# Two output projections done as one product of 2x2 blocks by seven multiplications

## The chip, the cores and the metric

The kernel runs on one core of one Trainium2 chip. The metric is the device time of one execution in microseconds (us), as the median of several runs. The profile shows the engines of the core: TensorE (PE for its matmuls, PEld for its weight loads), VectorE (DVE), ScalarE (ACT), GpSimd (POOL) and SyncE (SP, whose queue issues DMAs). SBUF is the working memory with 128 partitions, and PSUM is the memory of eight banks into which TensorE writes.

## The reference

One layer of a decoder trunk over 2048 positions of 1024 features, all in float32:

```python
h = rms_norm(x, norm1_g)
proj = einsum('bsd,dc->bsc', h, w_in)              # 2048 columns
a_out = spatial_gating(u_a, v_a, ...)              # 512 features
b_out = conformer_conv(val_b, gate_b, ...)         # 512 features
mix = concatenate([a_out, b_out], axis=-1)
x = x + einsum('bsc,cd->bsd', mix, w_out)          # the output projection
h = rms_norm(x, norm2_g)
f = square(relu(einsum('bsd,df->bsf', h, w_ff1)))  # 4096 features
x = x + einsum('bsf,fd->bsd', f, w_ff2)
return rms_norm(x, final_g)
```

The change is about the line of the output projection: a product of `mix` (2048 positions by 1024 features) with `w_out` (1024 by 1024), to which the residual `x` is added.

## The kernel before

**Tiles.** Activations lie transposed, with features on the partitions and positions along the free dimension. The positions are cut into four blocks of 512, numbered 0 to 3. Features and weight columns are cut into tiles of 128, so a block has 8 feature tiles (`KD`).

**Precision.** Every float32 operand is split into a high part, cast by ScalarE to a reduced form (fp32r), and a low part, which is the operand less its high part. A product of two split operands is three matmuls (`mm3`, line 179): high by high, high by low, low by high. The low part is computed by `rest` (line 163). It goes to GpSimd or to VectorE, whichever the kernel's own planner picks. The planner is a set of clocks, one for each engine, that advance by an assumed cost per instruction. `rest` takes GpSimd as long as its clock is less than `GPS_LEAD[0]` ahead of TensorE's clock, or more than 2 behind VectorE's. `GPS_LEAD` is 5.0 at first and 1.5 from line 1045.

**Memory.** Nearly all operands live in one pool of 41 slots of 128 x 1024 float32 (`slot`, `slot2`); smaller temporaries live in a pool of ten (`tmp`). An instruction that writes a new tile waits until a slot is free. DMAs are issued mostly by the queue of SyncE, in order.

**Order.** The changed stages stand under `manual_schedule`, so each engine gets its instructions in the order in which the program text makes them. Work that is to come some steps later is put into a list by `later(n, f)` and made by `beat()`, which is called once a step. `beside()` and `tick()` put bits of other work (such as the preparation of the down projection's weights, W2) beside a step: `pace["w2"]` says how many W2 items are begun for each call. An item is one prepared weight operand: a sum on VectorE (for four kinds in seven), a cast on ScalarE, a low part, and a DMA to DRAM.

**Stages.** The input projections and mixers of the four blocks come first, with the output projections of blocks 0 and 1 between them (`stage_o(0)`, `stage_o(1)`). The mixer's results of blocks 2 and 3 are stored in DRAM (`p_d`). Then come:

- u0, the first matrix of the MLP for blocks 0 and 1 together (`multiply("u0", ...)`, 112 steps);
- `stage_o(2)` and `stage_o(3)`, the output projections of blocks 2 and 3;
- u1, the same as u0 for blocks 2 and 3;
- the second matrix of the MLP, in 16 chunks (`down_chunk`).

u0, u1 and the down chunks already multiply by seven products. Two blocks of positions and two halves of the contracted and of the output features make a 2x2 by 2x2 block product. Seven products of sums of blocks give it, in place of eight. `BANK` (line 775) says in which bank a product is accumulated, and `INTO` (line 778) to which output block the bank's content is added when the product is done. The operands of u0 and u1 that come from the residual stream are called hops (`hop`, line 922): 28 slots for each pair of blocks, each made from `xr`, the residual after the output projection, by a scaling or a sum, a cast and a low part.

**The output projection of one block** (`stage_o`, line 645) runs over 8 output tiles `d`. Each takes one PSUM bank and contracts 8 feature tiles, 3 matmuls each: 192 matmuls of 128x128 weights by 512 positions. Weight tiles of 1024 columns come from `w_o` through `load_w`, `w_hi` and `w_lo`, two output tiles ahead. Both blocks load and split all of them. The mixer's results are brought back by `reload` (line 1007) and split into `mix[b]`. The result is added to the residual by VectorE (`evict`), stored as `x1_d`, and squared by ScalarE, and the squares are summed by GpSimd (`square_add`) for the second norm (`row_scale`). Beside `stage_o(2)`, 16 calls of `beside` with a pace of 0.2 make W2 items; beside `stage_o(3)` the hops of products 1, 2, 5 and 6 of u1 are made (`first_at`).

## Time and profile before

| What | Value |
|---|---|
| Median of 3 runs | 1831.97 us (1828.97 to 1837.33) |
| Profiled execution, its own time | 1831.89 us |
| Its span, first to last instruction | 1830.2 us |
| Granted TensorE clock, mean | 0.997 of full speed |
| DMA traffic | 424.74 MB, 232 GB/s over the span |

Lines of a group view read: line of the program, engine, operation, tile written <- tiles read, shapes, count | busy us, mean ns of one | idle time of the engine just before, and what ended it. Line 78 is the helper through which the planner's engines issue, so groups are told apart by their tiles: `po` is the bank of the output projection, `py`, `pz`, `px` are those of the seven-product stages, `w_hi`, `w_lo`, `m_hi`, `m_lo` the split operands. In the view of waits, a line gives who waited, for whom, us in total, times, and the longest. Matmuls are pipelined, so their durations overlap.

### The profile page before, as it was taken

To read this page: it belongs to the slowest core of one execution; us is meant where nothing else is said; L and a number is where in the kernel's file an instruction comes from. 1 tells how busy PE (TensorE), PEld (TensorE's weight loads), DVE (VectorE), ACT (ScalarE), POOL (GpSimd) and SP (SyncE) were. 2 spreads that over 40 slices of the span, in tenths; PEclk is the share of its full clock that TensorE was granted. 3 is DMA by queue.
4 is the path that set the end of the run, shared out by engine and by line. 5 is a ranking of instruction groups with operands and counts; after the bars stand their busy time and mean duration, and the time that the engine had idled before them with its cause. 6 is when DMAs were issued, how large, how long until landed. Compare 5 with 4: busy or idle time off the path is not lost. (4 is left out here: it accounts for less than half of the span.)

```text
span 1830.2 us, 23249 instructions
## 1 busy us (share of the span) xinstructions
PE 1809.3 (99%) x8080; PEld 1488.5 (81%) x8080; DVE 1330.8 (73%) x1825; ACT 758.6 (41%) x1172; POOL 1233.3 (67%) x775
## 2 busy tenths in 40 slices
PE   9999999999999999999999999999999999999998
PEld 6888878888888888888888888888788888888886
DVE  5699997997998985632567787676866568665655
ACT  6345565454445445455354545432322231212112
POOL 4575975883766666699878989776945465444434
PEclk9999999999999999999999999999999999999999
DMA  8342655432645456685557778998987679767652
GB/s 327 112 164 91 229 178 213 184 125 83 220 150 189 161 195 202 215 293 204 208 184 266 270 258 298 355 408 335 412 326 248 252 272 327 299 238 256 254 191 93
DMA packets 131686, 424.74 MB, mean 232 GB/s; under 512 B 14576, under 2 KB 15216, under 8 KB 131568
## 3 DMA queue, kind: packets, MB, share of 16 engines
q1 hardware_dynamic: 96000, 329.12, 50.5%
q10 hardware_dynamic: 35568, 94.13, 13.2%
q8 instruction: 64, 1.05, 0.2%
q14 instruction: 54, 0.44, 0.1%
HBM read 302.60 MB, written 120.59 MB: 231 GB/s over the span
## 5 line engine op out<-in xcount | busy, mean ns | idle before, releaser
L78 PE MATMUL py<-fo_hi,w2o 128*128 128x512 f32 x1792 | 555.9, 391 | 0.8 <-DVE x L78 0.8
L78 POOL TENSOR_TENSOR fo_lo<-fraw,fo_hi 128x1024 fp32r<-128x1024 f32 x111 | 274.4, 2481 | 252.9 <-ACT fo_hi L160 210.7
L78 DVE TENSOR_TENSOR x<-py,x 128x512 f32<-128x512 f32 x448 | 300.9, 687 | 185.8 <-PE py L78 185.4
L78 PEld LDWEIGHTS py<-fo_hi,w2o 128*128 128x128 f32 x1792 | 337.1, 188 | 72.0 <-DVE x L78 1.2
L78 PE MATMUL py<-hop,w1o 128*128 128x512 f32 x1536 | 363.8, 390 | 0.5 <-ACT c L982 0.4
L78 PE MATMUL py<-fo_lo,w2o 128*128 128x512 f32 x896 | 349.7, 390 | 0.9 <-POOL fo_lo L78 0.8
L78 PEld LDWEIGHTS py<-hop,w1o 128*128 128x128 f32 x1536 | 287.6, 188 | 62.4 <-issue 1.4
L78 DVE SCALAR_TENSOR_TENSOR acc<-g,vec,acc 128x512 f32<-128x512 f32 x464 | 322.9, 746 | 1.2
L160 ACT CAST fo_hi<-fraw 128x1024 fp32r<-128x1024 f32 x112 | 117.0, 1052 | 413.7 <-PE py L78 218.0
L78 POOL TENSOR_TENSOR w_lo<-raw,w_hi 128x1024 fp32r<-128x1024 f32 (+1 forms) x94 | 224.1, 2392 | 53.9 <-ACT w_hi L160 39.6
L78 POOL TENSOR_TENSOR w1o<-wraw,w1o 128x512 fp32r<-128x512 f32 x120 | 172.0, 1438 | 55.6 <-ACT w1o L810 43.4
L78 PEld LDWEIGHTS py<-fo_lo,w2o 128*128 128x128 f32 x896 | 168.6, 188 | 37.9 <-POOL fo_lo L78 2.6
L78 PE MATMUL pz<-hop,w1o 128*128 128x512 f32 x768 | 183.8, 390 | 0.0
L78 POOL TENSOR_TENSOR w1o<-ws,w1o 128x512 fp32r<-128x512 f32 x90 | 128.7, 1433 | 66.4 <-ACT w1o L810 62.6
L78 PEld LDWEIGHTS pz<-hop,w1o 128*128 128x128 f32 x768 | 143.8, 188 | 29.8
L78 DVE TENSOR_TENSOR fraw<-fraw 128x1024 f32<-128x1024 f32 x64 | 93.1, 1455 | 13.3 <-POOL fo_lo L78 13.2
L993 ACT ACTIVATE c<-c 128x512 f32<-128x512 f32 x128 | 80.8, 631 | 52.5 <-DVE c L78 52.0
L78 PE MATMUL po<-m_hi,w_hi 128*128 128x512 f32 x256 | 101.1, 395 | 0.0
L78 PE MATMUL po<-m_hi,w_lo 128*128 128x512 f32 x256 | 99.8, 390 | 0.6 <-POOL w_lo L78 0.6
L78 PE MATMUL po<-m_lo,w_hi 128*128 128x512 f32 x256 | 99.7, 389 | 0.0
L78 DVE TENSOR_TENSOR px<-px,c 128x512 f32<-128x512 f32 x32 | 22.3, 698 | 100.9 <-PE px L78 67.8
L78 POOL TENSOR_TENSOR w2p<-wraw,w2p 128x512 fp32r<-128x512 f32 x64 | 93.5, 1463 | 2.6 <-ACT w2p L810 2.6
(155 smaller groups left out, 2947.9 us busy)
## 6 DMA issues: line engine op xcount, KB each, us to landing
w2o<-w_d SPq DMA_DIRECT2D x224, 512.0 KB, 6.0
w_d<-w2p ACTq DMA_DIRECT2D x112, 512.0 KB, 5.4
wraw<-in_w SPq DMA_DIRECT2D x92, 512.0 KB, 4.7
f_d<-c ACTq DMA_DIRECT2D x128, 256.0 KB, 4.1
fraw<-f_d SPq DMA_DIRECT2D x64, 512.0 KB, 6.8
raw<-in_w_ct SPq DMA_DIRECT2D x48, 512.0 KB, 5.0
raw<-in_w_o SPq DMA_DIRECT2D x32, 512.0 KB, 5.4
w1o<-w_d SPq DMA_DIRECT2D x28, 512.0 KB, 5.5
```

What stands on the lines that cost most here:

```text
L78: return op(out, *args, **kwargs)
L160: nc.scalar.copy(hi, src)
L993: later(1, lambda: nc.scalar.activation(c, c, AF.Square))
```

## The change

`stage_o(2)`, `stage_o(3)`, `reload` and what belongs to them are taken out. In their place stands one loop, `stage_o_pair`, which computes both blocks as a product of 2x2 blocks by seven products. It takes its weights from a second arrangement of the same matrix, `w_o2`. The rows of the 2x2 are the parities of the feature tiles, the columns the two blocks (`t` = 0 is block 3, `t` = 1 is block 2). The contraction over four pairs of feature tiles, `q`, is the inner loop: step `n` is product `i` and depth tile `q`, 28 steps, in each of which all four output tiles `j` of the product get 12 matmuls. PSUM is reopened with all eight banks before the loop, and again as six and two after it.

```diff
-    def reload(b):
...
+    ORDER_O = (1, 5, 6, 3, 7, 2, 4)
+    OP = [(i, q) for i in ORDER_O for q in range(4)]
+    DONE = {3: (0, 1), 7: (1, 1), 2: (0, 0), 4: (1, 0)}
...
+    def op_hi(n):
+        if not 0 <= n < len(OP):
+            return
+        i, q = OP[n]
+        while ("m", q, 0 if i == 1 else 1) not in op:
+            op_load()
+        r11, r12 = [op["w", q, 0][:, a * 512:a * 512 + 512] for a in range(2)]
+        if i != 1:
+            r21, r22 = [op["w", q, 1][:, a * 512:a * 512 + 512] for a in range(2)]
+            if i == 5 and q % 2 == 0:
+                op["s", q // 2] = slot("osum")
+            s = op["s", q // 2][:, q % 2 * 512:q % 2 * 512 + 512]
+            if i == 5:
+                dsb.tensor_tensor(s, r21, r22, op=ALU.add)
+            elif i == 6:
+                dsb.tensor_tensor(s, s, r11, op=ALU.subtract)
+            elif i == 3:
+                dsb.tensor_tensor(s, r12, s, op=ALU.subtract)
+            elif i == 7:
+                dsb.tensor_tensor(r21, r11, r21, op=ALU.subtract)
+        lsrc = r11 if i == 1 else {2: r12, 4: r22, 5: s, 6: s, 3: s, 7: r21}[i]
+        bt = [op["m", q, t] for t in range(2 if i != 1 else 1)]
+        if i == 1:
+            rsrc = bt[0][:, :512]
+        else:
+            rsrc = right([[t[:, a * 512:a * 512 + 512] for t in bt] for a in range(2)], i, 0)
+        for side, src in (("l", lsrc), ("r", rsrc)):
+            o = slot2("of")
+            nc.scalar.copy(o[:, 0, :], src)
+            op[side, n] = (src, o)
+
+    def op_lo(n):
+        if 0 <= n < len(OP):
+            for side in "lr":
+                src, o = op[side, n]
+                rest(src, o[:, 0, :], o[:, 1, :])
+
+    def op_out(i, j, ps):
+        a, t = INTO[i]
+        b, d = 3 - t, 2 * j + a
+        x_ = xr[b][d]
+        dve.tensor_tensor(x_, ps, x_, op=ALU.add)
+        if DONE.get(i) == (a, t):
+            nc.sync.dma_start(
+                x1_d[b, j][:, a * 512:a * 512 + 512], xt1[b][j][:, a * 512:a * 512 + 512])
...
+    def stage_o_pair(at):
+        bks = {}
+        for n, (i, q) in enumerate(OP):
+            kind, first = BANK[i]
+            op_lo(n + 3)
+            op_hi(n + 4)
+            op_load()
+            ol, orr = op["l", n][1], op["r", n][1]
+            for j in range(4):
+                if first and q == 0:
+                    bks[kind, j] = mm_tile("po")
+                ps = bks[kind, j]
+                mm3(ps, [ol[:, k, j * P:(j + 1) * P] for k in range(2)],
+                    [orr[:, k, :] for k in range(2)], first and q == 0, q == 3)
+                if q == 3 and n == 27:
+                    op_out(i, j, ps)
+                elif q == 3:
+                    later(1, lambda j=j, ps=ps, i=i: op_out(i, j, ps), True)
+            beat()
+            at(n)
+
+    def at_o(n):
+        if 20 <= n < 24:
+            hop(1, 1, n - 20)
+        if 22 <= n < 26:
+            hop(1, 2, n - 22)
+        if n >= 26:
+            hop(1, 5, 2 * n - 52)
+            hop(1, 5, 2 * n - 51)
+        if n == O_LEAD[0]:
+            GPS_LEAD[0] = O_LEAD[1]
+        if n == 27:
+            GPS_LEAD[0] = 1.5
...
-    mid = reopen_banks(early, "m", mm=6, tp=2)
+    mid = reopen_banks(early, "o", mm=8)
...
-        stage_o(2, at_o2)
...
-        stage_o(3, first_at(1))
+        stage_o_pair(at_o)
+    mid = reopen_banks(mid, "m", mm=6, tp=2)
```

The function `right`, which was there for the down projection, makes the sum on the right side (one subtraction for products 5, 6, 7 and 4, in place). `op_load` issues the 24 loads of 512 KB (8 of weights, 8 of mixer results, 8 of the residual) on the queue of SyncE. It is called twice a step from step 102 of u0 on, and once a step in the loop. In the last four steps of u0 the operands of steps 0 to 3 are made.

`O_LEAD` is (14, -6.0): from step 14 to step 27 the planner's lead for GpSimd is -6.0, so that `rest` goes to VectorE unless GpSimd's clock is well behind. The hops of product 6 move from `stage_o(3)` into the first steps of u1 (`REST`, now one list for each pair of blocks). W2 items that were begun are finished in the first steps of the loop, and none is begun in it. `row_scale` gets two arguments for its delays.

More of the change, by code (lines that the diff above doesn't have):

```diff
@@ L149, in tp_tile @@
     def tp_tile(name):
-        return bank("tp", name)
+        return bank("tp" if "tp" in banks else "mm", name)
     def tiny(name, n=4):
@@ L1005, in reopen_banks @@
         return st
-    def reload(b):
-        p = parts[b]
-        g = p.reload()
-        def load(n):
-            while p.pairs[n] is None:
-                next(g)
-                if p.pairs[n] is None:
-                    yield
-        yield from load(0)
-        yield
-        yield from load(1)
-        yield
-        for k in range(KD):
-            if k % 2 == 0:
-                pair = halves(act_pair("m"))
-                yield from load(min(k // 2 + 2, 3))
-            nc.scalar.copy(pair[k % 2][0], p.at[k])
-            later(1, lambda k=k, hl=pair[k % 2]: rest(p.at[k], *hl))
-            mix[b].append(pair[k % 2])
-            yield
     def at_up0(n):
@@ L1102, in right, with op_loads, w, m @@
         return {1: b11, 2: b21, 5: b11, 6: b11, 7: b12, 3: b22, 4: b11}[i]
+    ORDER_O = (1, 5, 6, 3, 7, 2, 4)
+    OP = [(i, q) for i in ORDER_O for q in range(4)]
+    op = {}
+    DONE = {3: (0, 1), 7: (1, 1), 2: (0, 0), 4: (1, 0)}
+    def op_loads():
+        def w(q, a):
+            op["w", q, a] = slot("oraw")
+            nc.sync.dma_start(op["w", q, a], w_o2[q, a])
+        def m(q, t):
+            op["m", q, t] = slot("mraw")
+            nc.sync.dma_start(
+                op["m", q, t].rearrange("p (a t) -> p a t", a=2), p_d[1 - t, q])
+        for t in range(2):
+            for q in range(4):
+                w(q, t)
+                yield
+                m(q, t)
+                yield
+            for q in range(4):
+                load_resid(3 - t, q)
+                yield
@@ new lines, in hybrid_block_kernel, with op_load @@
+    op_gen = op_loads()
+    def op_load(n=1):
+        for _ in range(n):
+            next(op_gen, None)
+    def op_hi(n):
[28 more added lines that the diff above has]
+            op[side, n] = (src, o)
@@ new lines, in hybrid_block_kernel @@
+    count = [0, 0]
+    def stage_o_pair(at):
[18 more added lines that the diff above has]
+            at(n)
@@ new lines, in hybrid_block_kernel, with load_x1 @@
+    GPS_LEAD[0] = 1.5
+    dve.time += BEHIND
+    with tc.manual_schedule():
+        stage_o(1, first_at(0))
+        multiply("u0", UNITS, 0, up_out(0), at_up0)
+    mid = reopen_banks(early, "o", mm=8)
+    del banks["tp"]
+    gst.close()
+    more["w2"] = pool(sb, "more", 3)
+    pace["w2"] = 0.0
+    with tc.manual_schedule():
+        stage_o_pair(at_o)
+    mid = reopen_banks(mid, "m", mm=6, tp=2)
+    dn = {"x": [[] for _ in range(NB)]}
+    def load_x1(b, kp):
+        x = slot("x1")
+        nc.sync.dma_start(x, x1_d[b, kp])
+        dn["x"][b] += [x[:, 0:512], x[:, 512:1024]]
```

104 lines of the change are left out of this document (48 added, 56 removed).

## The prediction

> **What bounds the kernel now.** I read the page's engine table first, then the list of what TensorE waited for, then the tile view of the old output projection, and last the stage windows and the timelines of VectorE and GpSimd.
>
> ```profile
> span 1830.2 us, 23249 instructions
> PE 1809.3 (99%) x8080; PEld 1488.5 (81%) x8080; DVE 1330.8 (73%) x1825; ACT 758.6 (41%) x1172; POOL 1233.3 (67%) x775
> ```
>
> ```profile
> PE sgu L78 <- ACT gv L585: 3.0, 1, 3.0
> ...
> PE po L78 <- POOL w_lo L78: 0.6, 1, 0.6
> ```
>
> The reader is to see that TensorE is busy for 99% of the span, and that its longest wait anywhere is 3.0 us. In the stage that is changed it waits once, for 0.6 us. So the kernel's time is its number of matmuls times their pitch, and a matmul less is time less as long as its operands are ready.
>
> ```profile
> L78 PE MATMUL po<-m_hi,w_hi x128: 389/389/793, 796.6 to 885.6; 128*128 128x512 f32 x128
> L78 PE MATMUL po<-m_lo,w_hi x128: 387/389/396, 796.8 to 885.9; 128*128 128x512 f32 x128
> L78 PE MATMUL po<-m_hi,w_lo x128: 389/389/499, 797.0 to 886.1; 128*128 128x512 f32 x128
> ```
>
> ```profile
> 709.52 2.88 PE L78 MATMUL px<-hop,w1o 128*128 128x512 f32 x12
> 712.24 2.88 PE L78 MATMUL py<-hop,w1o 128*128 128x512 f32 x12
> ```
>
> The first fence is the tile view of the two projections that are changed: 384 matmuls between 796.6 and 886.1 us. The mean of 389 ns isn't their price, because they overlap. The price is the distance of their starts: twelve start in 712.24 - 709.52 = 2.72 us, which is 0.2267 us each. 384 of these are 87.0 us; the stage's 89.5 us hold besides the 0.6 us wait and the small matmuls of the row sums. Whoever takes 389 ns for a matmul gets a gain that is 1.7 times too large.
>
> ```profile
> 755.00:796.50 41.50, 41.50 (x185) 34.37 (x184) 20.38 (x26) 23.34 (x40) 29.31 (x22) 1.00 0.72 242
> 796.50:886.50 90.00, 89.41 (x396) 73.47 (x396) 28.50 (x27) 41.87 (x63) 86.30 (x55) 1.00 0.65 230
> 930.00:1180.00 250.00, 249.93 (x1103) 206.33 (x1102) 179.66 (x175) 132.28 (x241) 219.61 (x148) 1.00 0.75 274
> 1180.00:1320.00 140.00, 138.31 (x605) 112.88 (x604) 109.19 (x127) 46.72 (x63) 106.45 (x55) 1.00 0.97 385
> ```
>
> The columns are the stretch, its length, then the busy us of PE, PEld, DVE, ACT, POOL. In the changed stage (second row) GpSimd is busy for 86.3 of 90 us and VectorE for only 28.5. GpSimd is near to being the next bound there, and VectorE has room.
>
> **The change part by part.**
>
> *Matmuls.* The new loop has 28 steps of 4 x 3 = 12 matmuls, 336 in place of 384. The shapes stay 128x128 by 128x512, so the pitch stays: 48 x 0.2267 = **-10.9 us**. The wait for w_lo goes with the loop that had it: **-0.6 us** (between 0 and 0.6). One step is 2.72 us of PE; due times below count from the loop's first matmul.
>
> *Preparation.* Rows of the old stage, from its groups by shape:
>
> ```profile
> L78 POOL TENSOR_TENSOR w_lo<-raw,w_hi 128x1024 fp32r<-128x1024 f32 x14 | 33.4, 2394 | 0.0
> L78 POOL TENSOR_TENSOR sq<-sq 128x512 f32<-128x512 f32 x12 | 16.3, 1361 | 1.4 <-ACT sq L482 1.3
> L78 POOL TENSOR_TENSOR m_lo<-part,m_hi 128x512 fp32r<-128x512 f32 x10 | 13.2, 1331 | 0.0
> L78 DVE TENSOR_TENSOR xr<-po,xr 128x512 f32<-128x512 f32 x15 | 10.3, 687 | 44.1 <-PE po L78 39.3 <-DMA w_d<-w2p 4.7
> L1026 ACT CAST m_hi<-part 128x512 fp32r<-128x512 f32 x8 | 4.9, 610 | 0.0
> ```
>
> Before, 16 weight tiles of 1024 columns and 16 mixer tiles of 512 are split, in halves of 512 columns 32 + 16 = 48. After it is 28 x 2 = 56 halves, each a ScalarE cast (0.61 us) and a remainder subtraction (1.33 us on GpSimd). New are 32 VectorE sums (16 on the left for products 5, 6, 3, 7, and 16 on the right for 5, 6, 7, 4), and 28 evictions in place of 16 (12 x 0.69 = 8.3 us of VectorE more). ScalarE stays easy: 56 x 0.61 = 34 us in a loop of 28 x 2.72 = 76 us, beside squares and hops. What sums and remainders cost each other is read from the next stage's timelines, first GpSimd, then VectorE:
>
> ```profile
> 1006.90 1.74 POOL L78 TENSOR_TENSOR w1o<-wraw,w1o 128x512 fp32r<-128x512 f32 x1
> 1008.60 1.75 POOL L78 TENSOR_TENSOR w2p<-wraw,w2p 128x512 fp32r<-128x512 f32 x1
> ...
> 1012.00 1.30 POOL L78 TENSOR_TENSOR w2p<-wraw,w2p 128x512 fp32r<-128x512 f32 x1
> 1013.25 1.30 POOL L78 TENSOR_TENSOR w1o<-ws,w1o 128x512 fp32r<-128x512 f32 x1
> ```
>
> ```profile
> 1005.71 1.78 DVE L78 TENSOR_TENSOR ws<-wraw,ws 128x512 f32<-128x512 f32 x1
> 1007.41 1.78 DVE L78 TENSOR_TENSOR wraw<-wraw 128x512 f32<-128x512 f32 x1
> ```
>
> ```profile
> 770.97 1.28 DVE L78 TENSOR_TENSOR wraw<-wraw 128x512 f32<-128x512 f32 x2
> 772.17 1.28 DVE L78 TENSOR_TENSOR ws<-wraw,ws 128x512 f32<-128x512 f32 x2
> ```
>
> Alone, GpSimd starts one each 1.25 us (1012.00, 1013.25) and VectorE one each 0.60 us (two from 770.97 to 772.17). Side by side both start one each 1.70 us. So a pair costs 1.70 us, little less than 1.25 + 0.60 = 1.85 one after the other.
>
> The Trainium skill (SBUF — State Buffer, "Who interferes with whom") says that a VectorE instruction with two SBUF inputs and a GpSimd one that reads SBUF hold one port pair exclusively, so that the loser blocks. By that rule a pair costs the full 1.85 us; the rows show 1.70, and the sum goes by the rows. The rule's own result is the second rival.
>
> *Does it keep pace?* Up to step 14 the kernel's planner sends remainders to GpSimd (its lead there is +1.5). For products 5 and 6, and for 7 later, a step needs two sums and two remainders, 2 x 1.70 = 3.4 us, while PE takes 2.72. I follow operands by step number, all sums at 1.70.
>
> ```profile
> 791.12 5.60 PE L78 MATMUL py<-hop,w1o 128*128 128x512 f32 x24
> 796.56 0.39 PE L78 MATMUL po<-m_hi,w_hi 128*128 128x512 f32 x1
> ```
>
> ```profile
> 796.76 0.69 DVE L78 SCALAR_TENSOR_TENSOR c<-py,r_rows 128x512 f32<-128x512 f32 x1 [2.03 <-DMA part<-p_d]
> ```
>
> Operands 0 to 3 (no sums) are made in u0's last steps, where GpSimd has 12 of 41.5 us free. The first sum stands on VectorE behind u0's last eviction: 796.76 + 0.69 is 0.9 after the loop's start. Sums 4 to 7 end at 0.9 + 8 x 1.70 = 14.5, their remainders after 1.2 of casts and 2 x 1.25 at 18.2; step 7 is due at 19.0, in time. Now four evictions of product 1 (2.8 us) hold VectorE to 17.3. Sums of operand 8 end at 19.6 (one contended, one alone), then one operand each 3.4; with 0.6 for a cast and 3.0 for two remainders they are ready at 23.2, 26.6, 30.0, 33.4, due 21.8, 24.5, 27.2, 29.9: late by 1.4 growing to 3.5. Operand 12 comes behind four more evictions: 29.8 + 2.8 + 1.4 + 0.6 + 3.0 = 37.6 against 32.6 + 3.5 = 36.1, 1.5 more, and three steps of 1.70 + 1.25 = 2.95 add 0.2 each: **5.7 us late by step 15**. From step 14 on the lead of -6 moves remainders to VectorE; four operations of 0.60 and an eviction are 3.1 us for the two steps that still have two sums, later ones need at most 2.5, and the loss ends.
>
> The other end is 0: in the third window row the same planner feeds PE with some 1.65 remainders a step (one w1o, 0.65 w2p) with GpSimd busy for 88%, and PE loses 0.07 us of 250. Each stretch in which one of the two engines waits for PE runs the other at its lone price. I take **+3.0 us**, about the middle, and keep 0 and 9.5 (worked out with the rival).
>
> *Loads and stores.*
>
> ```profile
> raw<-in_w_o SPq DMA_DIRECT2D x32, 512.0 KB, 5.4
> part<-p_d SPq DMA_DIRECT2D x8, 512.0 KB, 4.7
> ```
>
> 16 weight loads become 8, the mixer and residual loads stay, 8 stores of 512 KB become 16 of 256 KB: 4 MB less, in a stage with DMA busy 0.65. The first are asked for six steps, 16 us, ahead of their use and land in 5.4: nothing while slots are free (without slots: rival 3).
>
> *Banks.* All eight banks are reopened at both ends of the loop. Four banks are now filled in 2.72 us, where one bank took 5.4. u0's last read of a bank ends at 797.45, 0.9 us after the loop's first matmul, so the hand-over costs 0 to 0.9 us each time, by which bank comes first. I take **+0.4** for both together (ends 0 and 1.8).
>
> *W2 work put off.* The old stage ran 16 x 0.2 = 3.2 W2 items beside itself; the new loop only finishes those begun, so three more fall to the down projection.
>
> ```profile
> 1289.21 1.73 POOL w2p L78
> 1290.93 2.38 POOL fo_lo L78
> ...
> 1293.36 196.83 PE py L78 x867
> ```
>
> ```profile
> L905 ACTq DMA_DIRECT2D w_d<-w2p x28: 326/326/362, 1203.0 to 1318.3; - x28
> ```
>
> There GpSimd ends last until 1293, yet PE loses only 140 - 138.3 = 1.7 us. If all three remainders came on that path, 3 x 1.73 = 5.2 us; if the same share of the 28 items that are done there, 3/28 x 1.7 = 0.2. The chain leaves GpSimd soon, so **+0.3**, ends 0 and 5.2.
>
> *Hops to the second up projection.* Products 1 and 2 now start their hops at steps 20 and 22, 5 at step 26, and 6 goes into u1 itself, each two to four steps ahead of its use. 16 of them in nine steps are 1.8 a step: with one sum (three of four kinds) and a remainder each, 1.8 x 1.70 = 3.0 us at most against 2.72, with evictions beside. The two or more steps of lead cover that, 0 (at worst 4 steps' worth of the excess and an eviction each, 4 x 1.0 = 4 us).
>
> Sum: -10.9 - 0.6 + 3.0 + 0.4 + 0.3 = -7.8 us. The profiled execution took 1831.9 us (span 1830.2 and 1.7 around it), which is the median of the runs, 1832.0, to 0.1. Forecast **1824.1 us**.
>
> **The rivals.**
>
> 1. *All of the preparation is hidden.* For it speaks u1's 0.07 us of idle, and that operands lead by four steps. Against it, 3.4 us of pairs per step in steps 0 to 7. Time: 1831.9 - 11.5 + 0.7 = **1821.1**.
>
> 2. *Sums and remainders exclude each other fully.* An operand with two sums then takes 2 x 1.85 = 3.7 in place of 3.4; twelve of those add 3.8 to the 5.7, so 9.5 are lost and the gain is all but gone: 1831.9 - 11.5 + 9.5 + 0.7 = **1830.6**. The pitch of 1.70 speaks against it, GpSimd's 86 of 90 us for it. This is what the rule of the Trainium skill named above gives. A late head of u1 (4 us, hops) ends near here too.
>
> 3. *Slots run dry, and the time gets longer.* Loads hold 24 of the 41 slots, two hold sums, and each operand two; four steps of lead are 34, the rest is for up- and W2 operands in flight. Queue SP waited for a slot before, too:
>
> ```profile
> SPq L364 <- PE py L78: 13.2, 1, 13.2
> ```
>
> If fewer than two operands fit ahead, the work runs in series: two sums (1.2), two casts (1.2), two remainders (2.5) are 4.9 us a step, 2.2 over PE's 2.72. Over the twelve two-sum steps, 26 us: 1831.9 - 11.5 + 26 = **1846**. It makes the kernel slower by 0.5% once nine or ten steps run so. Against it: the 28 hop slots of u0 come free in the very steps in which the loads are asked for.
>
> **How the numbers follow.** Forecast (1 to 5 us lost) 0.40; all hidden 0.30; full exclusion or a late u1 0.23; slots 0.07. A difference of 0.5% (9.2 us, below 1822.8 or above 1841.1) is about what a measurement of this kernel tells from no change. All of rival 1 and a quarter of the forecast case fall below that: faster 0.40; slots: slower 0.07; the rest, 0.53, within. The range reaches from rival 1 with no cost at hand-overs (1820.4) to just past rival 2: 1820.0 to 1832.5. It leaves out the slots and the worst of late hops.
>
> **What would show it.** The tile of the new products: 336 matmuls, and first to last start near 76 us if nothing waits, 79 by the forecast. PE's waits: remainders of the new operands in steps 8 to 15, none after 20. VectorE's sums at 1.7 us until step 14, near 0.6 after. Waits of PE for a DMA or of casts for slots would speak for rival 3; waits for hops in u1's first twelve steps for the late head. I am wrong in kind if the pitch isn't 0.2267, or if PE idles at a stage that I hold unchanged.

## The result, and the profile after

The changed kernel is slower. Its median of 6 runs is 1844.11 us (1839.68 to 1849.47), beside 1831.23 us (1828.97 to 1837.33) for 6 runs of the kernel before on the same chip: a ratio of 1.0064, with a 95% interval of 1.0045 to 1.0084. The forecast was 1824.1 us with a range to 1832.5. Both the sign and the range were wrong.

First the page of the changed kernel: its span, and the busy time, share and instructions of each engine.

```profile
span 1845.0 us, 23243 instructions
PE 1809.2 (98%) x8032; PEld 1483.9 (80%) x8032; DVE 1400.9 (76%) x1881; ACT 767.9 (42%) x1196; POOL 1253.9 (68%) x787
```

The 48 matmuls are gone (8032 in place of 8080), and VectorE is busy for 70 us longer. To see where the time went I take the first matmul of each stage from the tile views and compare the lengths of the stages. "Entry" is the first matmul of the first output projection, "loop" runs from the first matmul of the changed stage to the first of u1, "u1" from there to the first of the down projection, "down" from there to the start of the last matmul that writes `py` from `fo_hi`.

| Profiled execution | Span | Entry | Loop starts | Loop | u1 | Down |
|---|---|---|---|---|---|---|
| Before | 1830.2 | 298.3 | 796.6 | 89.7 | 307.0 | 621.4 |
| After | 1845.0 | 304.3 | 800.7 | 89.5 | 312.7 | 625.7 |
| After, run again | 1839.5 | 298.2 | 794.6 | 89.5 | 314.3 | 625.6 |
| Before, run again | 1828.6 | 299.3 | 796.4 | 89.8 | 307.0 | 619.9 |

The last two ran one after the other on one chip and enter at nearly the same time. Their difference of 10.9 us is -1.8 (start of the loop) - 0.3 (loop) + 7.3 (u1) + 5.7 (down). So two things have to be explained: **the loop has an eighth fewer matmuls and isn't shorter, and two stages behind it, whose program the diff hardly touches, are 13 us longer.** The 4.1 us by which the first pair differs ahead of the loop are not the change's; the last section shows where they arise.

The list of what TensorE waited for, in the kernel after (who, for whom, us in total, times, the longest):

```profile
PE ct L79 <- ACT c L306: 4.6, 1, 4.6
...
PE po L79 <- POOL of L79: 2.6, 7, 0.4
PE py L79 <- POOL hop L79: 2.6, 4, 0.9
PE py L79 <- ACT w2p L817: 2.4, 1, 2.4
PE ssum L79 <- DVE xr L79: 2.2, 1, 2.2
PE py L79 <- DVE x L79: 2.1, 2, 1.4
```

Before, a single wait stood in the changed stage, 0.6 us. Now the new loop waits seven times for operands from GpSimd (`of`) and once for a bank that VectorE frees late (`ssum`, released by `xr`). u1 waits for hops and the down projection for W2 operands. No wait is for a DMA. The timeline of TensorE in the loop shows what these cost (start, us, operation, idle before and what ended it):

```profile
800.70 24.90 PE L79 MATMUL po<-of 128*128 128x512 f32 x109
825.93 3.06 PE L79 MATMUL po<-of 128*128 128x512 f32 x12 [0.33 <-POOL of L79]
...
842.14 3.02 PE L79 MATMUL po<-of 128*128 128x512 f32 x12 [0.38 <-POOL of L79]
845.53 3.01 PE L79 MATMUL po<-of 128*128 128x512 f32 x12 [0.38 <-POOL of L79]
848.93 3.02 PE L79 MATMUL po<-of 128*128 128x512 f32 x12 [0.39 <-POOL of L79]
852.32 22.06 PE L79 MATMUL po<-of 128*128 128x512 f32 x95 [0.38 <-POOL of L79]
876.56 1.64 PE L79 MATMUL ssum<-ones,sq 128*128 128x1 f32 x8 [2.18 <-DVE xr L79]
878.06 11.00 PE L79 MATMUL po<-of 128*128 128x512 f32 x36
890.24 3.02 PE L79 MATMUL py<-hop,w1o 128*128 128x512 f32 x12 [1.17 <-DVE xr L79]
```

The distance of starts tells more than the idle time in brackets, since each wait also empties the matmul pipeline. From 842.14 on, steps start every 3.39 us in place of 2.72. The 205 matmuls ahead of 852.32 (48 of them in the rows left out) take 852.32 - 800.70 = 51.62 us, **5.1 us** more than 205 x 0.2267. The next 95 and the wait behind them take 24.24, 2.7 more. The eight small matmuls of the row sums take 1.50. The last 36 matmuls take 11.0 where 8.16 are due, 2.8 more, and 1.2 pass until u1. All of it: 336 x 0.2267 = 76.2, + 5.1 + 2.7 + 1.5 + 2.8 + 1.2 = 89.5 us, which is the loop.

Why 36 matmuls take 2.8 us too long is in the stretches of that time; the third number from the end of a line is the granted clock:

```profile
878.00:881.00 3.00, 3.00 (x8) 2.42 (x9) 2.09 (x4) 3.00 (x7) 3.00 (x3) 0.50 1.06 311
881.00:884.00 3.00, 3.00 (x9) 2.35 (x9) 0.69 (x1) 2.97 (x7) 3.00 (x3) 0.57 0.98 328
884.00:887.00 3.00, 3.00 (x15) 2.49 (x14) 2.60 (x2) 2.03 (x4) 3.00 (x3) 1.00 0.79 324
```

After the wait TensorE ran at half its clock until 883.6 us, which is 5.5 us of these matmuls, then at full clock again.

What the engines beside it did, first VectorE in steps 5 and 6 and at the end of the loop, then GpSimd at the end:

```profile
815.55 0.68 DVE L79 TENSOR_TENSOR osum<-osum,oraw 128x512 f32<-128x512 f32 x1
816.15 1.78 DVE L79 TENSOR_TENSOR mraw<-mraw 128x512 f32<-128x512 f32 x1
817.85 1.78 DVE L79 TENSOR_TENSOR osum<-osum,oraw 128x512 f32<-128x512 f32 x1
...
870.65 1.78 DVE L79 TENSOR_TENSOR mraw<-mraw 128x512 f32<-128x512 f32 x1
872.35 1.78 DVE L79 TENSOR_TENSOR of<-oraw,of 128x512 fp32r<-128x512 f32 x1
874.05 1.76 DVE L79 TENSOR_TENSOR mraw<-mraw 128x512 f32<-128x512 f32 x1
875.74 2.47 DVE L79 TENSOR_TENSOR xr<-po,xr 128x512 f32<-128x512 f32 x4
```

```profile
868.44 6.82 POOL L79 TENSOR_TENSOR sq<-sq 128x512 f32<-128x512 f32 x4
```

A sum takes VectorE 0.68 us where GpSimd doesn't hold it up (815.55), and 1.78 us where it does. The second is the rule in steps 5 and 6, and still is in the last steps: of the loop's 56 remainders nine moved to VectorE, all of them after 847 us (`of` at 872.35), GpSimd kept the others and was adding squares between them, and these collide with VectorE in the same way. So the four evictions of product 2 (875.74) came late, and the row sums, which needed one of the eight banks, waited for them.

The stretches of the loop and of u1's head after, and u1's head before (busy PE, PEld, DVE, ACT, POOL):

```profile
800.70:889.20 88.50, 83.59 (x345) 65.42 (x343) 84.68 (x72) 44.07 (x77) 88.03 (x56) 0.96 0.33 121
890.20:912.00 21.80, 20.59 (x90) 16.24 (x91) 17.40 (x17) 12.33 (x22) 21.25 (x16) 1.00 0.70 253
```

```profile
886.40:908.00 21.60, 21.60 (x99) 17.66 (x98) 13.20 (x14) 12.36 (x22) 15.40 (x12) 1.00 0.70 249
```

In the loop VectorE and GpSimd are now both full (84.7 and 88.0 of 88.5 us), and GpSimd carries its backlog into u1, where it is busy for 21.25 of 21.8 us (before 15.40 of 21.6).

### The profile page after: what moved, and what is told of

Its sections match the earlier page's. It is cut to its first block, busy times and chain, and to the rows that moved or that the text cites. A ratio compares the mean times of both kernels' runs of the same rounds, so it can differ in the third digit from the quotient of the medians.

```text
span 1845.0 us, 23243 instructions
## 1 busy us (share of the span) xinstructions
PE 1809.2 (98%) x8032; PEld 1483.9 (80%) x8032; DVE 1400.9 (76%) x1881; ACT 767.9 (42%) x1196; POOL 1253.9 (68%) x787
## 3 DMA queue, kind: packets, MB, share of 16 engines
q8 instruction: 63, 1.03, 0.2%
## 4 chain that ended last, share of the span: by engine, by line
PE 80%; DVE 10%; DMA 3%; POOL 3%; issue 2%; ACT 1%; SPq 0%; POOLq 0%; ACTq 0%; DVEq 0%
PE py L79 46%; PE pz L79 9%; PE po L79 5%; PE px L79 4%; PE pg L79 4%; PE pu L79 4%; PE pv L79 3%; DVE acc L79 3%; PE pvv L79 3%; DMA w2o<-w_d 2%; DVE xr L79 1%; DVE mraw L79 1%; POOL fo_lo L79 1%; DMA raw<-in_w_v 1%; DVE osum L79 1%
## 5 line engine op out<-in xcount | busy, mean ns | idle before, releaser
L79 POOL TENSOR_TENSOR fo_lo<-fraw,fo_hi 128x1024 fp32r<-128x1024 f32 x111 | 278.5, 2518 | 257.4 <-ACT fo_hi L162 216.3
L79 PEld LDWEIGHTS py<-fo_hi,w2o 128*128 128x128 f32 x1792 | 337.1, 188 | 76.2 <-DVE x L79 2.9
L79 POOL TENSOR_TENSOR w_lo<-raw,w_hi 128x1024 fp32r<-128x1024 f32 (+1 forms) x79 | 188.2, 2391 | 54.5 <-ACT w_hi L162 37.8
L79 POOL TENSOR_TENSOR sq<-sq 128x512 f32<-128x512 f32 x53 | 77.1, 1456 | 23.3 <-ACT sq L1364 13.8
L79 PE MATMUL px<-hop,w1o 128*128 128x512 f32 x384 | 91.7, 389 | 0.0
L79 PE MATMUL po<-of 128*128 128x512 f32 x336 | 82.1, 403 | 2.6 <-POOL of L79 2.6
```

Of the source, the lines that this page charges most:

```text
L79: return op(out, *args, **kwargs)
```

## The experiments

My theory at this point: **the engines that prepare operands are the bound in the loop, through the collision of VectorE and GpSimd, and what they leave undone costs u1 and the down projection.** The rivals: the loop is held by something else (banks, a slower pitch in a loop with all eight banks); u1 and down are longer by chance, as the start of the execution is; the W2 items put off are what lengthens down. The first four ran one after the other on one chip, with runs of the kernel before between them; so did the next four, the next four, then two, one and two. The table behind the experiments holds all of their times.

**The same kernels again**, with no edit.

> The changed kernel once more, for where its time goes from execution to execution. In the first profile it enters the output projection of block 0 at 304.3 us, 6.0 later than before, although the instructions up to there are the same in the same order on every engine; there a 128x4 VectorE instruction took 6.7 us in place of 1.8 beside back-to-back GpSimd work. If that is chance, this profile enters that stage between 298 and 304 at another value, while the loss in the new loop (89.5 us for 336 matmuls), in the head of the second up projection and in the down projection stays. If it comes from the change (another input, other addresses), it is 304 again.

> The kernel before once more, one look, for the same question: if the early 6.0 us are chance, the kernel before can show some of them too (entry into the projection of block 0 anywhere from 298 to 304), and its own stage of two projections stays at 89.8 us from first matmul to the next stage. If they belong to the change, the entry is at 298 again.

Measured: 1843.94 us, ratio 1.0064 (1.0046 to 1.0083), and 1830.27 us for the one execution of before. The loop has 89.5 us again, u1 and down are longer again, and these belong to the change. The early 4 us are not there. The 1344 matmuls of u1 are 304.7 us at the pitch; u1 takes 9.6 us more than that here and 2.3 more before. Of these, 2.6 us are idle time at four waits for hops and 0.4 at one for squares. Down holds, beside smaller waits:

```profile
1297.14 0.47 PE L79 MATMUL py<-fo_hi,w2o 128*128 128x512 f32 x1 [2.40 <-ACT w2p L817]
```

```profile
1298.00:1300.00 2.00, 2.00 (x7) 1.52 (x6) 2.00 (x5) 0.66 (x2) 2.00 (x2) 0.50 1.18 352
```

The first line is from the timeline, the second a stretch behind it: here too the clock is at 0.50 after the wait. In the first profile of the same kernel a wait of 2.41 us stands at the same place (1301.74), the clock stays at 1.00 behind it, and down takes 625.7 us all the same.

**No sums.** The 32 sums on VectorE are left out, each product multiplying one block in place of a sum.

```diff
-            if i == 5:
-                dsb.tensor_tensor(s, r21, r22, op=ALU.add)
...
-        lsrc = r11 if i == 1 else {2: r12, 4: r22, 5: s, 6: s, 3: s, 7: r21}[i]
+        lsrc = r11 if i == 1 else {2: r12, 4: r22, 5: r21, 6: r21, 3: r12, 7: r21}[i]
...
+            rsrc = {5: b11, 6: b11, 7: b12, 3: b22, 2: b21, 4: b11}[i]
```

> Leaves out all 32 sums of the new loop: products 5, 6, 7, 3 and 4 get unsummed blocks. Theory (a sum and a low part cost 1.70 us as a pair, so a step with two of each takes 3.4 us against 2.72): the waits of 0.38 us at each step from 8 to 16 go, 5 us, and the loop takes 84 us or less from its first matmul to the first of the next stage; if VectorE is then also in time at the end, the wait before the row sums and the slow clock after it go too, and it takes 77 us. Rival (slots or loads hold the preparation): the loop stays at 87 to 90 us, with casts or loads waiting.

Measured: 1833.19 us, ratio 1.0001 (0.9980 to 1.0021). The tile view of the products, first of this kernel, then of the kernel after:

```profile
L79 PE MATMUL po<-of x336: 387/390/485, 803.9 to 880.8; 128*128 128x512 f32 x168
```

```profile
L79 PE MATMUL po<-of x336: 387/389/774, 800.7 to 888.7; 128*128 128x512 f32 x168
```

First to last start is 76.9 us in place of 88.0, and the loop 77.1. This is what 336 matmuls cost with all operands ready, 12.6 us less than the stage before. The 32 sums take nearly the whole of it (12.4) away. They are not to be had for nothing, so this shows the most that the loop can gain and is no version of the kernel. u1 (314.5) and down (626.1) stay long: what lengthens them isn't the sums.

**W2 items beside u0.** The pace of W2 in u0 is raised, so that the items which the loop no longer takes are made there.

```diff
-W2_PACE = (0.3, 0.2, 0.65, 0.7)
+W2_PACE = (0.34, 0.2, 0.65, 0.7)
```

> The pace of W2 items beside the first up projection is 0.34 in place of 0.3: 3.4 items more there, about those that the new loop no longer makes. Theory (the 3.7 us that the down projection lost more than before, 1185 to 1350 us, come from the items put off): TensorE's waits there fall from 6.4 us to the 2.7 of the kernel before, and the time falls by 3 to 4 us. Rival (they come from the late entry or from other transfers): the waits stay at 5 to 7 us and the time falls by under 1 us.

Measured: 1840.09 us, ratio 1.0034 (1.0015 to 1.0053). Down falls to 619.3 us, and its waits for `w2p` and `x` are gone; loop and u1 stay.

**Remainders on VectorE alone, for steps 4 to 15**, so that GpSimd has nothing to collide with there.

```diff
-                rest(src, o[:, 0, :], o[:, 1, :])
+                if 4 <= n < 16:
+                    dsb.tensor_tensor(o[:, 1, :], src, o[:, 0, :].bitcast(F32), op=ALU.subtract)
+                else:
+                    rest(src, o[:, 0, :], o[:, 1, :])
```

> The low parts of steps 4 to 15 of the new loop go to VectorE, so GpSimd is idle there. Theory (side by side a VectorE and a GpSimd operation start one each 1.70 us, VectorE alone one each 0.60; the pair is what sets the pace): a two-sum step takes 4 x 0.60 + 0.69 = 3.1 us in place of 3.4 and the lead of four steps covers what is over 2.72; the seven waits of 0.38 us and their 5.0 us of excess from step 8 to 16 go, and the loop falls from 89.5 to about 84.5 us. Rival (the number of operations on both engines is too large, whoever does them): VectorE is now alone with all of it, the waits get longer, and the loop takes 92 us or more.

Measured: 1860.62 us, ratio 1.0168 (1.0140 to 1.0197). The waits of steps 8 to 15 are gone; no wait stands ahead of 843.9 (step 16). But from there on the planner, which now counts VectorE as late, sent the remainders to GpSimd, behind the squares: waits of 3.9 and 4.8 us in the loop, 4.2 at its end and 7.2 in u1. Undoing one part only moved the load.

**The same for steps 4 to 27.** The bound of the condition is 28.

> The low parts of steps 4 to 27 all go to VectorE. Theory: as the run with steps 4 to 15 up to step 16; after it GpSimd has only the squares and hops, 1.25 each, so that VectorE's evictions at step 23 come in time for the bank of the row sums: the wait of 2.2 us and the half clock behind it (2.9 us) go too, and the loop takes 78 to 80 us. Rival (from step 16 on VectorE with 2 low parts, a sum and an eviction, slowed by the squares beside it, is the bound): the wait before the row sums is 2 us or longer.

Measured: 1846.81 us, ratio 1.0082 (1.0063 to 1.0101), loop 88.6 us. VectorE's timeline in step 6, with two remainders and two sums:

```profile
810.73 0.69 DVE L79 TENSOR_TENSOR of<-osum,of 128x512 fp32r<-128x512 f32 x1
811.33 0.69 DVE L79 TENSOR_TENSOR of<-mraw,of 128x512 fp32r<-128x512 f32 x1
811.94 0.68 DVE L79 TENSOR_TENSOR osum<-osum,oraw 128x512 f32<-128x512 f32 x1
812.54 0.68 DVE L79 TENSOR_TENSOR mraw<-mraw 128x512 f32<-128x512 f32 x1
```

They start 0.60 us apart, four in 2.4 us: VectorE alone makes a whole step's operands in less than the 2.72 us of the step, while both engines together need 3.4. That is the collision, taken away and measured. GpSimd stood idle for 47 us, and then its squares fell together with sums and remainders at the end. A wait of 4.2 us for the bank of the row sums and one of 8.0 us in u1 for squares gave it all back.

**Row sums one step later**, to let product 2's bank come free first.

```diff
-                    later(4, row_scale(b, 2, 1 + t))
+                    later(5 if t else 4, row_scale(b, 1 if t else 2, 1 + t))
```

> The row sums of block 2 are issued one step (2.72 us) later, the rest in the loop as it was. Theory (the sums need a bank that VectorE frees 2.2 us late, and the eight one-column matmuls after that idle leave TensorE so empty that it runs at half clock for some 5 us): TensorE has a step's matmuls to do meanwhile, the 2.2 us wait goes, no slice of the loop has a clock of 0.5, and the loop falls from 89.5 to 84 to 85 us. Rival (VectorE is late for good by then, so the lateness is only moved): the wait of 2 us stands before another matmul and the loop stays within 1 us of 89.5.

Measured: 1843.84 us, ratio 1.0065 (1.0041 to 1.0089), loop 89.5. The wait for the bank is gone. In its place stand 2.4 us for an operand (`of`) and 2.5 for a bank at u1's first matmul. The half clock is there as well (871.95 to 875.36, behind the wait for the operand), with no one-column matmul ahead of it. The row sums were only the first to meet a late VectorE.

**Hops on VectorE.** The remainders of the hops of products 5, 6 and 7 go to VectorE, which had 4.4 of 21.8 us free in u1's head while GpSimd was full.

```diff
-            rest(src, o[:, 0, :], o[:, 1, :])
+            if pair and i in (5, 6, 7):
+                dsb.tensor_tensor(o[:, 1, :], src, o[:, 0, :].bitcast(F32), op=ALU.subtract)
+            else:
+                rest(src, o[:, 0, :], o[:, 1, :])
```

> The low parts of u1's hops of products 5, 6 and 7 go to VectorE. Theory (u1's head is late since GpSimd has squares and hop low parts in one row from 887 to 920 us while VectorE stands idle for 5 us at a time): the waits for hop low parts (2.6 us in four) go, and u1 falls from 313 to 314 us to 309 or less. Rival (the hops of product 6 come too late in the program, whoever does them): the waits stay, now for VectorE, and u1 stays above 312.

Measured: 1838.21 us, ratio 1.0022 (1.0002 to 1.0043). u1 falls from 314.3 to 309.9 us, and of four waits for hops one of 0.28 us is left. In u1's head GpSimd is now busy for 9.70 of 22 us:

```profile
890.00:912.00 22.00, 21.85 (x99) 17.53 (x98) 19.45 (x27) 15.46 (x28) 9.70 (x6) 1.00 0.64 234
```

So 4.4 of u1's 7.3 us were GpSimd's backlog.

**Both of these, and what the loop can be given.** Four kernels follow: W2 beside u0 and the hops together; with that all remainders and block 2's squares on VectorE; in place of these, VectorE for the remainders of steps 4 to 19 and one remainder for each engine in steps 20 to 27; and W2's pace alone in the kernel before.

```diff
-                square_add(acc[b], x_)
+                square_add(acc[b], x_, eng=dsb if t else gps)
```

```diff
+                if 4 <= n < 20 or (n >= 20 and side == 'l'):
+                    dsb.tensor_tensor(o[:, 1, :], src, o[:, 0, :].bitcast(F32), op=ALU.subtract)
+                elif n >= 20:
+                    gps.tensor_tensor(o[:, 1, :], src, o[:, 0, :].bitcast(F32), op=ALU.subtract)
```

> The two single edits outside the loop together: hop low parts of products 5, 6 and 7 on VectorE, and 0.34 for the W2 pace beside u0. Theory (three losses that stand side by side, in the loop, in u1's head and in the down projection): the loop stays at 89.5 us, u1 takes some 310 and the down projection some 619, which is 89.5 + 310 + 619 = 1018.5 against 89.8 + 307 + 620 to 621 = 1017 to 1018 of the kernel before, so the time is that of the kernel before within 0.2%. Rival (the losses hang together, and what one gives back the next stage loses): the time stays some 0.3% above.

> The same two edits, and in the loop the low parts of steps 4 to 27 and the sums of squares of block 2 on VectorE. Theory (VectorE alone starts one each 0.60 us; 32 sums, 48 low parts, 7 sums of squares, 28 evictions of 0.60 are 69 us of a loop of 76): the squares no longer slow the low parts at step 16, the waits behind step 16 go, the loop takes 78 to 81 us, and the time falls to 8 us or more below the run with the two edits alone, below the kernel before by 0.4%. Rival (VectorE has no room left, any waiting for a cast is lost): the loop stays at 86 to 89 us, and there is no gain over the kernel before.

> The same two edits, and in the loop the low parts of steps 4 to 19 on VectorE; from step 20 the left low part on VectorE and the right one on GpSimd, squares on GpSimd. Theory (pairs at 1.70 are what costs): like the run with all on VectorE up to step 16, then the pairs with squares slow VectorE, and a wait of 2 us or more with the half clock behind it comes back before the row sums: loop 84 to 88 us. Rival (VectorE alone is the bound, GpSimd's help counts): the loop is shorter than with all on VectorE, 80 us or less.

> The kernel before with a W2 pace of 0.34 in place of 0.3 beside the first up projection, to tell what of the gain of that edit belongs to the change. Theory (the down projection's extra waits come from the items that the new loop doesn't make): the kernel before had them made in its projections, so it gains 2 us at most, its down projection taking 618 to 621 us. Rival (the down projection is short of W2 items in either kernel): it gains 4 us or more, as the changed kernel did.

Measured: ratios 1.0008 (0.9993 to 1.0024), 1.0013 (0.9996 to 1.0029), 1.0018 (1.0004 to 1.0032) and 1.0027 (1.0013 to 1.0041). The first repairs what lay behind the loop, and lands on the kernel before. It also shows what the half clock is worth there. The end of its loop, and the clock in it:

```profile
872.62 1.02 PE L79 MATMUL ssum<-ones,sq 128*128 128x1 f32 x8 [2.17 <-DVE xr L79]
873.51 8.80 PE L79 MATMUL po<-of 128*128 128x512 f32 x36
886.26 4.50 PE L79 MATMUL py<-hop,w1o 128*128 128x512 f32 x12 [3.95 <-DVE xr L79]
```

```profile
874.00:877.00 3.00, 3.00 (x14) 2.45 (x14) 2.16 (x4) 3.00 (x7) 3.00 (x3) 1.00 1.04 315
```

Behind nearly the same wait as in the kernel after, 2.17 us, the clock stayed full, and the last 36 matmuls took 8.8 us in place of 11.0. Yet the loop has 89.5 us again: what the clock gave, the wait for VectorE at u1 took (3.95 us in place of 1.17). The second kernel shortens the loop to 86.9 us only: VectorE is busy for 71.3 of the 76.5 us up to 878, and the rest is waits for it, 3.5 us of it for the bank of the row sums. The third kernel gains nothing in the loop (89.3). The last is a surprise: the pace that shortened down in the changed kernel lengthens it in the kernel before, from 619.9 or 621.4 to 626.0. So down isn't simply short of W2 items; how its work falls together matters as much.

**A quarter of the remainders back on GpSimd, beside the evictions.** Product evictions read a bank and the residual, so only one of their inputs lies where GpSimd's do. So remainders of every fourth step, which fall beside evictions, go to GpSimd, all else as in the second kernel above. A second kernel has W2's pace put back to 0.3.

```diff
+                if n >= 4 and n % 4 != 3:
+                    dsb.tensor_tensor(o[:, 1, :], src, o[:, 0, :].bitcast(F32), op=ALU.subtract)
+                elif n >= 4:
+                    gps.tensor_tensor(o[:, 1, :], src, o[:, 0, :].bitcast(F32), op=ALU.subtract)
```

> As the run with all low parts and block 2's sums of squares on VectorE, but the low parts of every fourth step (3 modulo 4 from step 7 on) go to GpSimd: they become ready when VectorE evicts four banks from PSUM, 2.4 us in which two GpSimd operations of 1.25 us don't meet it. Theory (pairing sets the pace, not capacity): VectorE has 12 x 0.60 = 7.2 us less to do, its waits from step 18 on go, the loop takes 77 to 81 us, and the time falls 5 us or more below that run, below the kernel before by 0.2 to 0.5%. Rival (the chain of sum, casts and low part within the lead of four steps is the bound): the loop stays at 85 to 88 us.

> The same with the W2 pace of 0.3 beside u0, as in the kernel before. Theory (the items that the new loop doesn't make are missed in the down projection): the loop is the same within 1 us, the down projection takes 624 to 626 us in place of 619 to 621, and the time is 4 us longer. Rival (how the down projection falls out depends on the stages before it, not on three items): it takes 619 to 622 us here too.

Measured: ratios 0.9997 (0.9978 to 1.0017) and 1.0015 (0.9997 to 1.0034), loops 84.7 and 85.3 us. The timelines of GpSimd and of VectorE in the first of them:

```profile
843.45 1.31 POOL L79 TENSOR_TENSOR of<-oraw,of 128x512 fp32r<-128x512 f32 x1 [9.28 <-ACT of L1109]
844.71 1.31 POOL L79 TENSOR_TENSOR of<-mraw,of 128x512 fp32r<-128x512 f32 x1
```

```profile
843.19 2.48 DVE L79 TENSOR_TENSOR xr<-po,xr 128x512 f32<-128x512 f32 x4
```

Side by side, the remainders take 1.31 us and four evictions 2.48, both at their lone price. In the loop one wait of 1.7 us for an operand and one of 3.5 for the bank of the row sums are left.

**The row sums later once more**, now that nothing else is late there (the edit shown above, on the first of these kernels); then with that the hops of products 1 and 2 on VectorE too, or those of 2 alone.

```diff
-            if pair and i in (5, 6, 7):
+            if pair and i in (1, 2, 5, 6, 7):
```

> The run with every fourth step's low parts on GpSimd, and the row sums of block 2 one step later. Theory (VectorE is now late only around step 23, by the squares, and catches up after it): the wait of 3.5 us before the row sums falls to 1 us, the slow clock behind it goes, the loop falls from 84.7 to 79 to 81 us and the time by 4 us, to 0.2% below the kernel before. Rival (VectorE is late for good): the wait moves, as in the earlier run with the same edit, and the loop stays at 84 to 86 us.

> As the run before with the row sums later, and the low parts of u1's hops of products 1 and 2 on VectorE too. Theory (u1's head waits for GpSimd, which has squares and hops in one row): the waits for hop low parts go, u1 falls from 316 to 310 us, the loop stays at 80 to 82, and the time is 0.3 to 0.5% below the kernel before. Rival (VectorE has no room at the end of the loop): the loop grows by what u1 gains, the time stays within 0.2% of the kernel before.

> The same with the hops of product 2 alone moved besides (product 1's stay on GpSimd), half the step: between the two by either theory; by the first, u1 at 310 to 313 us and the loop at 80; by the rival, the sum of both stages as in the run before within 1 us.

Measured: ratios 0.9989 (0.9974 to 1.0005), **0.9973 (0.9957 to 0.9988)** and 0.9984 (0.9971 to 0.9997), loops 80.1, 79.2 and 80.1 us. The second is the fastest version, 1828.00 us beside 1832.21 for the kernel before on that chip, 0.27% less (0.12% to 0.43%). That is under the 0.5% named with the prediction, but 12 and 23 runs make the interval narrow enough to leave out no change. It is the fastest of thirteen edited versions and wasn't measured a second time, so its 0.27% may owe something to the choice. Its loop is 10.5 us shorter than before, and u1 takes 6.7 of that back. Its group of the largest sums, beside the same group of the kernel after (both from the stretch 796 to 890):

```profile
L79 DVE TENSOR_TENSOR mraw<-mraw 128x512 f32<-128x512 f32 x16 | 11.8, 735 | 0.0
```

```profile
L79 DVE TENSOR_TENSOR mraw<-mraw 128x512 f32<-128x512 f32 x16 | 27.1, 1692 | 0.0
```

The same sixteen sums cost 735 ns in place of 1692. TensorE's timeline in it:

```profile
796.50 65.67 PE L79 MATMUL po<-of 128*128 128x512 f32 x289
863.84 5.54 PE L79 MATMUL po<-of 128*128 128x512 f32 x23 [1.67 <-DVE of L79]
869.22 0.95 PE L79 MATMUL ssum<-ones,sq 128*128 128x1 f32 x8
870.03 5.75 PE L79 MATMUL po<-of 128*128 128x512 f32 x24
...
880.87 1.12 PE L79 MATMUL rbc<-dg,ones 128*128 128x512 f32 x2 [2.12 <-DVE dg L79]
881.43 4.92 PE L79 MATMUL py<-hop,w1o 128*128 128x512 f32 x12
```

24 steps pass without a wait. Then u1 waits for the row scale, 2.12 us, and runs slowly behind it; u1 has 313.7 us.

| Kernel | Median us | Ratio to before, 95% | Loop | u1 | Down |
|---|---|---|---|---|---|
| No sums (work left out) | 1833.19 | 1.0001 (0.9980-1.0021) | 77.1 | 314.5 | 626.1 |
| W2 beside u0 | 1840.09 | 1.0034 (1.0015-1.0053) | 89.5 | 313.4 | 619.3 |
| Remainders 4-15 on VectorE | 1860.62 | 1.0168 (1.0140-1.0197) | 97.0 | 322.0 | 624.0 |
| Remainders 4-27 on VectorE | 1846.81 | 1.0082 (1.0063-1.0101) | 88.6 | 320.6 | 625.4 |
| Row sums later | 1843.84 | 1.0065 (1.0041-1.0089) | 89.5 | 314.0 | 625.3 |
| Hops on VectorE | 1838.21 | 1.0022 (1.0002-1.0043) | 89.5 | 309.9 | 623.2 |
| W2 and hops | 1835.42 | 1.0008 (0.9993-1.0024) | 89.5 | 310.3 | 621.0 |
| with remainders, squares on VectorE | 1835.66 | 1.0013 (0.9996-1.0029) | 86.9 | 311.2 | 621.0 |
| with remainders divided by side | 1835.59 | 1.0018 (1.0004-1.0032) | 89.3 | 309.2 | 619.4 |
| Before, with W2's pace | 1838.47 | 1.0027 (1.0013-1.0041) | 89.7 | 307.8 | 626.0 |
| every fourth step on GpSimd | 1831.63 | 0.9997 (0.9978-1.0017) | 84.7 | 311.7 | 621.1 |
| the same, W2's pace as it was | 1835.47 | 1.0015 (0.9997-1.0034) | 85.3 | 309.7 | 623.7 |
| every fourth, row sums later | 1830.93 | 0.9989 (0.9974-1.0005) | 80.1 | 316.3 | 619.4 |
| with hops 1 and 2 on VectorE | 1828.00 | 0.9973 (0.9957-0.9988) | 79.2 | 313.7 | 620.9 |
| with hops 2 on VectorE | 1829.07 | 0.9984 (0.9971-0.9997) | 80.1 | 313.9 | 621.0 |

## Why the prediction was wrong

The matmuls came as forecast. What failed is the preparation: its +3.0 us in the loop with the claim that the loss ends at step 14, the 0 for the hops, and the +0.3 for the W2 items. Against the forecast of -7.8 us, the pair of executions with equal entry shows +10.9. The 18.7 us between them are 7.8 in the loop (-8.1 forecast, -0.3 measured), 7.3 in u1 (0 forecast), 5.4 in down (0.3 forecast, 5.7 measured), less 1.8 ahead of the loop.

**Matmuls: right.** Without the sums, 336 of them go through at 0.2267 us each, and the stage is 12.6 us shorter: 10.9 for the matmuls, 0.6 for the wait that is gone, and most of the rest for two matmuls of a row scale (`rbc`, some 0.9 us), which stood in the old stage at 861.0 and now stand in u1. That last part is only moved.

**The price of a pair: right.** Side by side the engines start one each 1.70 us, and the steps came at 3.39 us where 2 x 1.70 = 3.4 was worked out. The walk gave "5.7 us late by step 15"; measured are 5.1 at step 17. The second rival's 1.85 us didn't appear; its sum has a slip besides, since twelve times 0.3 us are 3.6 and not 3.8. (The Trainium skill, SBUF — State Buffer, "Who interferes with whom", has the loser block for the whole instruction, which by the estimate of the prediction gives 1.85; the rows of both kernels show 1.70.) The failed step here is the choice: I had walked operand by operand to 5.7, from rows of the same two engines at the same shapes, and then took +3.0 "about the middle" between that and 0. The 0 came from a stage with some 1.65 remainders a step, where the steps in question have two, and two sums. The walk was the nearer row, and the middle had nothing for it.

**"From step 14 on ... the loss ends": wrong.** I took it that the lead of -6 moves the remainders to VectorE. The planner moved nine of 56. Its rule still sends a remainder to GpSimd when GpSimd's clock is more than 2 behind VectorE's, which is the likely reason; its clocks are not in the trace. I also forgot that squares and hops stay on GpSimd. They collide with VectorE as remainders do: sums still took 1.78 us at 870.65. VectorE was therefore late with its evictions. With eight banks in use that is a wait for TensorE, 2.7 us at the row sums and 1.2 at u1, and 2.8 us between them by the half clock. The three are one lateness of VectorE: where the clock stayed full, the wait at u1 was longer by what the clock gave. Measured loss in the loop over its matmuls and row sums: 5.1 + 2.7 + 2.8 + 1.2 = 11.8 us, where the step had 3.0 and the banks 0.4 (their ends were 9.5 and 1.8).

**Hops: "0 (at worst ... 4 us)" was wrong.** I compared their number a step with TensorE's time and let two to four steps of lead cover the excess. But a lead covers a late start once, and GpSimd came out of the loop with a backlog. It was full for all of u1's head, VectorE wasn't, and the planner sent the remainders to GpSimd all the same. Moving the remainders of three products to VectorE takes 4.4 of the 7.3 us away. Of the other 2.9 some 0.9 are the two matmuls of the row scale, moved here from the old stage; the rest lies in small pieces and was not separated.

**W2: "+0.3, ends 0 and 5.2".** Down is 4.3 to 5.7 us longer, near or just past the upper end, and making the items beside u0 brings 6.3 of down back. The share of the items was a poor measure: TensorE waited 2.4 us for a single one (`w2p`). Why it came late was not taken apart; GpSimd, over which the quoted chain runs, was busy for only 101 of 140 us there (1185 to 1325). And the same pace lengthens down by 4.6 to 6.1 us in the kernel before, and between the two kernels that differ in it at a quarter of the remainders its worth is 2.6. That making the items earlier helps the changed kernel is shown. That their being put off is the whole cause isn't, and neither is a price for one.

**Rival 3 gave 1846 and is wrong nevertheless.** Its time is near the measured one, its mechanism didn't occur: no matmul waited for a load, and the operands came at the pace of the two engines, 3.4 us a step, not of the 4.9 of a chain in series. Loads and slots cost nothing, as forecast.

I named as wrong in kind "if PE idles at a stage that I hold unchanged". That is what happened, in two stages.

## What to carry to other kernels

A product saved by sums is paid for on the engines that make sums and remainders: here 10.9 us of matmuls against some 52 us of VectorE's time at the collided price. Before it is worth doing, add up all the work of both engines at that price, squares and hops among it, over the stage and the one behind it. If two engines collide, look at what one of them does alone before dividing the work: here VectorE alone made a step's four operations in 2.4 us, both engines side by side needed 3.4. Give one of them the operands, and the other what falls beside instructions that don't collide (1.31 and 2.48 us, both as alone). And where a walk from the nearest rows gives a number, use it, not the middle between it and a guess.

## What was unexpected of the hardware

**TensorE's clock falls for whole stretches of 3.41 us, and the wait's length alone doesn't decide it.** Behind the wait of 2.18 us in the loop the granted clock was at 0.50 from 876.8 to 883.6, behind 2.40 us in down from 1297.5 to 1300.9, behind 2.12 us in the fastest kernel from 882.2 to 885.6; there the twelve matmuls from 881.43 are followed at 886.18, after 4.75 us in place of 2.72. Where the row sums came without a wait, in the kernel without the sums on VectorE, the 36 matmuls behind them took 8.3 us (872.71 to 881.01), not 11.0. In the clock records of all nineteen traces, every stretch at 0.50 that ends before the trace does lasts 3.41 us, or twice or three times that. But behind 2.17 us in the run with W2 and hops, and behind 2.41 us in down of the kernel after, the clock stayed at 1.00, while behind 1.03 us and the row sums at 1497.88 in the fastest kernel it fell. The Trainium skill (TensorE: Matmul & The Clock Gate, "What's actually happening") puts the fall to half clock after an idle window of about 3.4 us. The length of the stretches agrees with such a window; that it must be idle throughout doesn't, since 2.12 us were enough. Where a wait lies in such a window may be what decides. Counted back in 64 steps of 3.413 us from the fall at 1518.5 in the kernel after, a border stands at 1300.0, inside the wait of 2.41 us that ends at 1301.74. No run moved a wait to test this. And a half clock need not cost time: with it and without it the loop took 89.5 us, and down took 625.6 us with it and 625.7 without.

**A small instruction of 6.7 us.** Executions of one program differ by some 5 us or more before the changed code is reached. The timelines of VectorE and of GpSimd in the profiled execution of the kernel after:

```profile
270.06 6.73 DVE L79 SCALAR_TENSOR_TENSOR nb<-mv,rs 128x4 f32<-128x4 f32 x1
```

```profile
269.42 2.38 POOL L79 TENSOR_TENSOR w_lo<-raw,w_hi 128x1024 fp32r<-128x1024 f32 x1
...
271.92 2.50 POOL L79 TENSOR_TENSOR m_lo<-part,m_hi 128x512 fp32r<-128x512 f32 x2
274.38 2.33 POOL L79 TENSOR_TENSOR w_lo<-raw,w_hi 128x1024 fp32r<-128x1024 f32 x1
```

A VectorE instruction of four columns takes 6.73 us and ends with the last of four GpSimd subtractions, with one short copy among them. In the kernel before, with the same neighbours, it ends with the first:

```profile
269.95 1.81 DVE L78 SCALAR_TENSOR_TENSOR nb<-mv,rs 128x4 f32<-128x4 f32 x1
```

TensorE's wait of 4.6 us for `c`, the longest in the list of the kernel after, follows behind it at 278.4. The five profiled executions that enter the first output projection at 303.6 us or later all have this instruction at 6.67 to 6.83 us and a wait for `c` of 3.4 to 4.6; the others enter at 301.0 or earlier and have it at 1.9 us or less. The kernel before with W2's pace is among the five, so it isn't the change. Such an instruction can be as long at another place without a late entry: 7.73 us at 221.1 in the run with the remainders of steps 4 to 15 on VectorE, which enters at 299.0. That VectorE lost its turn against GpSimd several times over is the likely reading; no run took it apart.
